# Attention in pairs of steps, the scans in two steps and the rotation back on GpSimd, in a hybrid MLA and S5 layer

## The chip, the cores and the metric

The kernel runs on one core of a Trainium2 chip. The metric is the time of one execution on the device in microseconds (us); lower is better. The engines are PE (TensorE), DVE (VectorE), ACT (ScalarE), POOL (GpSimd) and SP (SyncE, which issues most transfers). Each engine takes its instructions strictly in the order in which they are written, and waits for the others where data or a buffer is missing.

## The reference, cut to what matters

The layer takes x of 2048 positions by 1024 features in float32. After an RMS norm one product gives the inputs of two branches.

- Attention (MLA): four heads, a query of 128 features and 64 rotary ones for each, keys and values out of a common latent of 128 features, softmax over all 2048 positions.
- S5: 32 groups of 16 channels, each with a complex diagonal state of 64 in both directions; `h[t] = lam_bar h[t-1] + B u[t]`, `y = Re(C h) + D u`, then GELU and a gated unit.

```
s = einsum(qn, k_nope) + einsum(qr, k_rope);  p = softmax(s * scale);  o = p v
bu = einsum('sbgh,gph->sbgp', u, b_bar);  h = associative_scan(lam_bar, bu);  y += Re(einsum(h, c))
out = x + rmsnorm(concat(norm(o) * silu(g), norm(glu(gelu(y))) * silu(g2)) @ w_out)
```

## The kernel before

The program has three stages: the input product (phase 1), the attention loop with S5 beside it (phase 2), and the mixer with the output product (phase 3, `mixer`). The larger products take their operands in two parts, a high one in the type float32r and a low one, the rest.

The attention works on 32 units (`units`), a block of 256 queries by one head. A unit has eight steps: two halves of the queries (`qt`) by four blocks of 512 keys (`kb`). The loop over `t` runs these 256 steps and a tail of 15. In step `t` the queues receive, in this order:

- the second half of the row statistics of the last unit, if the step is the first of a unit (DVE: `L`, `lt`, `f`);
- `norm`: the exponentials of step t-9 are scaled (on ACT, L1143; on DVE, L1139, once the weights of phase 3 are being split);
- `s5_pre(t)`: what S5 has to do ahead of the scores;
- `scores`: five products into `sc` (PE, L1103 to L1107) and their maxima `nm` (DVE, L1108);
- `transp`: four transposes of step t-11 into `pt` (PE, L1151) and the high part `phi` (ACT, L1159);
- `expo`: `e` (ACT, L1114), in the last step of a unit the first half of the statistics;
- the low part `plo` (DVE, L1573);
- `av`: six products with the latent of step t-12 (PE, L1171 to L1173), after the eighth the copy `avs` (ACT, L1176); `unit_out` a step later;
- `s5_post(t)`, then a stage of the queries of the next block (`qprep`) or, near the end, of the weights of phase 3 (`out_weights`, `woh` on ACT at L1228).

A group of S5 is a routine (`group`) that goes one step at a time; a new group starts every seven steps, and takes fifteen. Its part around the change: the rotated inputs `ta`, `tb` (o = 6, counted from the group's start), their sum `X` (o = 7), four scans over 64 partitions each (o = 8, L1008 and L1009), the rotation back: `hc` on DVE (L1017) and `tb` on POOL (L1018) in o = 9, the difference `hc` on DVE (L1021) in o = 10, and PE's product with `hc` (L1034) in o = 14.

The rings that matter: score banks `psS` 2, transposes `psP` 2, `av` 1, `phi` and `plo` 2 each (`pp`), exponentials `e` 13 (`ep`). A new tile of a ring waits for the last reader of the one whose place it takes.

Of the kernel before, what the change touches and what calls it, by code (L numbers as in the profile page):

```python
# [21 lines left out]
P = 128  # L22
# [34 lines left out]
class Metered:  # L57
    """An engine that counts the elements it is given."""
# [13 lines left out]
class Scratch:  # L72
    """Temporaries of one shape, out of a ring of tiles of 512 (or, if small, 32) elements."""
# [22 lines left out]

def sincos(eng, sc, sin_out, cos_out, r):
    """sin and cos of r in about [-pi, pi], from those of r / 2."""
# [23 lines left out]
def exp_of(eng, sc, pool, out, x):  # L122
    """exp(x) in float32, exact at 0."""
# [24 lines left out]
def tile_hymba(ctx, tc, x, pos, inv_freq, pre_g, w_in, q_g, w_uqT, w_uqr, kv_g, w_ukT, w_uv, attn_g,  # L148
# [57 lines left out]
    # tables of the attention phase; those of S5 go through DRAM, by groups  # L206
# [11 lines left out]
    # ------------------------------------------------------------------ phase 1  # L218
# [51 lines left out]
    def turn(xt, t):  # L270
        """The tile's transpose, split, as tile t of a pair."""
# [34 lines left out]
    def gemm_t(nm, half):  # L306
        """Two blocks of 128 columns of a pair of tiles, with the columns in the partitions."""
# [43 lines left out]
    def s5_params():  # L351
# [37 lines left out]
        # F = (lam_bar - 1) / lam  # L389
# [17 lines left out]
        # powers of lam_bar, 0 .. T, in the order of each direction  # L407
# [29 lines left out]
        # phasors of chunk 32 i + 2 j + a: ph32 * (0..7) (+ phi), for a = 0, 1, and ph2 * (0..15)  # L437
# [13 lines left out]
        for nm, src in (("b", ph2), ("a", ph32)):  # L451
# [21 lines left out]
            # the backward direction turns the other way  # L473
# [11 lines left out]
        # B_bar = F B; B'' = B_bar e^{-i phi}; C' = lam_bar C  # L485
# [3 lines left out]
        def cm(orr, oi, ar, ai, xr_, xi_):  # L489
            """(orr, oi) = (ar + i ai)(xr + i xi), a over the last dimension."""  # L490
# [32 lines left out]
        # centre lag: Re(C B_bar) of both directions + D  # L523
        # (eight groups at a time: theirs are the blocks on the diagonal)
# [36 lines left out]
    def step():  # L561
        """A slice of the tables, of about BUDGET elements."""
# [15 lines left out]
    # absorbed weights: W_uq[h] W_uk[h]^T  # L578
# [23 lines left out]
    # the first tile is loaded and normed by halves  # L602
# [48 lines left out]
    # ------------------------------------------------------------------ phase 2  # L651
    # (the gate columns of the last two tiles run under its start)
# [5 lines left out]
    ep = pool(ph2, "ep", 13)  # L658
# [37 lines left out]
    # queries of a block of 256: each piece's last results are split a step later  # L696
# [74 lines left out]
    def both(*gens):  # L771
        """Step some routines in turn; what each returns."""
# [14 lines left out]
    # the gate columns of the last two tiles run under the start of the attention  # L787
# [58 lines left out]
    # S5  # L846
# [8 lines left out]
    def s5_load(q):  # L855
        """The tables of four groups."""
# [34 lines left out]
    def ops4(tile_, q_r, q_i, c1, c2):  # L891
        """The operands of tile_[., 2, s, h] = q_r[s] c1[., h] + q_i[s] c2[., h]."""
# [9 lines left out]
    def two(eng, tile_, tmp, *o):  # L902
        """The two products of a table; later they are added."""
# [18 lines left out]
    def k_build(q):  # L922
        """The kernels of the lags within a chunk, and their windows for each position."""
# [26 lines left out]
    def group(g):  # L950
        """A group of channels, a step at a time: what is ready first, what needs the PE last."""
        q, i = divmod(g, 4)
        f = S5[q]
        # (chunks in the order of their tiles: those of the even, then those of the odd places)
# [9 lines left out]
        # phasors over the chunks: -sin, cos, sin  # L964
# [39 lines left out]
        # (the states that enter the chunks; nothing enters the first, or the last backwards)  # L1004
# [6 lines left out]
        yield "pre"  # L1011
        yield "post"
# [4 lines left out]
        V.tensor_tensor(of_tiles(hc), g4, co, ALU.mult)  # L1017
# [3 lines left out]
        V.tensor_tensor(hc, hc, tb2, ALU.subtract)  # L1021
        yield "pre"
        yield "post"
# [20 lines left out]
    # when each group starts; the tables of the next four groups are made meanwhile  # L1044
# [52 lines left out]
    # attention  # L1097
    def scores(qo, st, i):
        qt, kb = i % 2, i // 2
        w = slice(qt * P, (qt + 1) * P)  # L1100
        c = slice(kb * 512, (kb + 1) * 512)
        ps = psS.tile([P, 512], F32, tag="s", name="sc")
        PE.matmul(ps, qo[:, 0, w], kT_h[:, c], start=True, stop=False)  # L1103
        PE.matmul(ps, qo[:, 0, w], kT_l[:, c], start=False, stop=False)  # L1104
        PE.matmul(ps, qo[:, 1, w], kT_h[:, c], start=False, stop=False)  # L1105
        PE.matmul(ps, qo[:, 2, w], krS[:, c], start=False, stop=False)  # L1106
        PE.matmul(ps, qo[:, 3, w], krS[:, c], start=False, stop=True)  # L1107
        V.tensor_reduce(st["nm"][:, qt, kb:kb + 1], ps, AX.X, ALU.max, negate=True)  # L1108
        st["s"] = ps

    def expo(st, i):
        qt, kb = i % 2, i // 2
        e = ep.tile([P, 512], F32, tag="e", name="e")
        A.activation(e, st.pop("s"), AF.Exp, bias=st["nm"][:, qt, kb:kb + 1], accum_out=st["L"][:, qt, kb:kb + 1])  # L1114
# [30 lines left out]
    def transp(st, j, tail=None):  # L1145
# [12 lines left out]
        ptf = pt.rearrange("p a b c -> p (a b c)")  # L1158
        A.activation(hi, ptf, AF.Copy)  # L1159
        st["p"][j] = hi, lo  # L1160
        return lo, ptf, hi
# [23 lines left out]
    # ------------------------------------------------------------------ weights of phase 3  # L1185
# [52 lines left out]
    # ------------------------------------------------------------------ phase 3  # L1238
    # (pairs of tiles, with the channels in the partitions up to W_out)
    def mixer():  # L1240
# [26 lines left out]
        def gelu(d):  # L1267
            """y <- 2 gelu(y), and its parts"""
# [38 lines left out]
        def part(d, src, h, c):  # L1307
            """hi and lo of half h of src, as blocks c .. of the products' operands"""
# [16 lines left out]
        def summed(d, sq):  # L1325
            """The sums of squares of the four channels in a partition"""
# [5 lines left out]
        def attn(d):  # L1332
            """o gated, and its parts"""
# [16 lines left out]
        def ssm(d):  # L1350
            """y <- 4 y sigmoid(. + b), gated into g, and its parts"""
# [37 lines left out]
        # the columns of the result in the parts that are worked on; the last tile ends in smaller ones  # L1389
# [11 lines left out]
        def comb(d, t, cs):  # L1401
            """Both branches by their factors, summed; the mean of the squares; times the gain"""
# [40 lines left out]
        # the first pairs, in small steps between those of the attention  # L1443
# [97 lines left out]
    late, qb = None, None  # L1541
    NLAG, LAG, AVLAG = 9, 11, 1
# [3 lines left out]
    TAIL = [[(0, "V"), (1, "A"), (2, "G"), (3, "G")], [(k, "G") for k in range(4, 8)]]  # L1546
    for t in range(8 * NU + LAG + AVLAG + 3):
        n, i = divmod(t, 8)
        # what the step before has made ready
        if n >= 1 and i == 0 and n - 1 < NU:  # L1550
            run(sts[n - 1]["stats"], 1)
        if t < 8 * NU and t >= NLAG:
            norm(sts[(t - NLAG) // 8], (t - NLAG) % 8, "A" if late is None else "V")
        s5_pre(t)
        # scores
        if n < NU:
            b, h = units[n]
            if i == 0:
                sts[n] = dict(e={}, p={}, nm=sm.tile([P, 2, 4], F32, tag="nm", name="nm"),
                              L=sm.tile([P, 2, 4], F32, tag="L", name="L"))  # L1560
            scores(qo[b][h], sts[n], i)
        m, j = divmod(t - LAG, 8)
        lo = transp(sts[m], j, p3) if 0 <= m < NU else None
        if n < NU:
            expo(sts[n], i)
            if t == 8 * NU - 1:
                V.tensor_tensor(lo[0], lo[1], f32(lo[2]), ALU.subtract)
                lo = None
            if i == 7:
                sts[n]["stats"] = stats(sts[n])  # L1570
                run(sts[n]["stats"], 1)
        if lo is not None:
            V.tensor_tensor(lo[0], lo[1], f32(lo[2]), ALU.subtract)  # L1573
        if t == 8 * NU - 1:
            norm(sts[NU - 2], 7, "V")
        elif 0 <= t - 8 * NU < len(TAIL):
            for k, eng in TAIL[t - 8 * NU]:
                norm(sts[NU - 1], k, eng)
        # (without scores in between, its operands take a step longer)
        lag = AVLAG + (t >= 8 * NU)  # L1580
        m, j = divmod(t - LAG - lag, 8)
        if 0 <= m < NU and t != 8 * NU:
            av(sts[m], j)
        m, j = divmod(t - LAG - lag - 1, 8)
        if 0 <= m < NU and j == 7:
            unit_out(*units[m], sts.pop(m))
        s5_post(t)
        # the queries of the next block
        if n < NU and b + 1 < 8:
# [89 lines left out]
```

## Time and profile before

| | us |
|---|---|
| median of 3 runs | 1434.57 (1433.16 to 1434.58) |
| span of the profiled execution | 1431.5 |
| attention loop, first to last exponential | 396.5 to 1170.6 |
| busy PE / DVE / ACT / POOL | 1359.6 / 1053.7 / 789.0 / 624.9 |

The profiled execution's own time is its span, from the first to the last instruction; the median of the runs lies 3.1 us above it. Matmuls overlap, so PE's busy time is not PE at its peak. An instruction's duration reaches some 0.08 us beyond the start of its neighbour on the same engine; what one costs is read from start to start.

### The profile page before, as it was taken

Reading aid. Unit: us, or ns where it says so; the run is one execution under the profiler, and the core shown is the slowest. Engines: PE = TensorE matmul, PEld = TensorE weight load, DVE = VectorE, ACT = ScalarE, POOL = GpSimd, SP = SyncE. Lnnn points to the kernel's source line nnn. Section 1 sums busy time; section 2 is a strip of 40 time slices with the busy share of each in tenths; the row PEclk is TensorE's granted clock in tenths of the full one; section 3 lists DMA queues with packets and bytes.
Section 4 is the critical chain, followed back from the end, with each engine's and each line's share of the span. In section 5 each row is a group of like instructions: output and inputs, shape, how many; then the busy total and the mean of one; then the engine's idle time right before and its main releaser. Section 6 shows DMA issues by size and latency. Waiting matters only on the chain.

```text
span 1431.5 us, 24291 instructions
## 1 busy us (share of the span) xinstructions
PE 1359.6 (95%) x9016; PEld 1221.6 (85%) x9016; DVE 1053.7 (74%) x1876; ACT 789.0 (55%) x1796; POOL 624.9 (44%) x616
## 2 busy tenths in 40 slices
PE   7999999999989999999999998999999989999998
PEld 7999999999968788887888887887888878788886
DVE  5456545332588888898989888988888895876774
ACT  6321222122457767767677676676677775544542
POOL 2102321233364655555556555645542695323340
PEclk9999999999999999999999999999999999999999
DMA  8322332442610110201102011020100345345432
GB/s 293 89 61 66 80 87 73 98 122 73 150 35 19 39 34 5 54 19 31 41 5 61 12 32 41 23 43 5 32 5 9 101 128 131 118 148 179 145 103 88
DMA packets 122133, 102.91 MB, mean 72 GB/s; under 512 B 14672, under 2 KB 107104, under 8 KB 122016
## 3 DMA queue, kind: packets, MB, share of 16 engines
q1 hardware_dynamic: 110384, 89.43, 22.3%
q0 software_dynamic: 2272, 7.62, 2.0%
q10 hardware_dynamic: 9360, 4.33, 1.5%
q8 instruction: 70, 1.15, 0.3%
q14 instruction: 47, 0.39, 0.1%
HBM read 63.80 MB, written 37.54 MB: 71 GB/s over the span
## 4 chain that ended last, share of the span: by engine, by line
PE 59%; DVE 26%; ACT 5%; issue 4%; POOL 2%; DMA 2%; SPq 1%; ACTq 0%; POOLq 0%; DVEq 0%
DVE plo L1573 5%; DVE nm L1108 4%; PE po L202 4%; PE po L203 4%; PE po L204 4%; PE pt L1151 3%; DVE hc L1017 3%; DVE G L1009 3%; DVE G L1008 3%; PE z_ga L203 2%; PE z_ga L204 2%; PE z_ga L202 2%; PE av L1173 2%; PE z_u L204 2%; PE z_u L202 2%
## 5 line engine op out<-in xcount | busy, mean ns | idle before, releaser
L1114 ACT ACTIVATE e<-sc,nm 128x512 f32<-128x512 f32 x256 | 176.4, 689 | 141.1 <-DVE nm L1108 139.8
L1573 DVE TENSOR_TENSOR plo<-pt,phi 128x512 fp32r<-128x512 f32 x255 | 175.0, 686 | 49.2 <-ACT phi L1159 46.3
L1159 ACT ACTIVATE phi<-pt 128x512 fp32r<-128x512 f32 x256 | 152.8, 597 | 72.9 <-PE pt L1151 72.4
L1108 DVE TENSOR_REDUCE nm<-sc 128x1 f32<-128x512 f32 x256 | 175.0, 683 | 17.6 <-PE sc L1107 15.6
L1173 PE MATMUL av<-plo,kn_h 128*128 128x256 f32 x512 | 150.6, 294 | 30.0 <-DVE plo L1573 29.5
L1171 PE MATMUL av<-phi,kn_h 128*128 128x256 f32 x512 | 165.7, 324 | 13.3 <-ACT avs L1176 13.2
L1143 ACT ACTIVATE e<-e,f 128x512 f32<-128x512 f32 x226 | 163.8, 725 | 1.5 <-DVE f L1132 1.5
L1151 PEld LDWEIGHTS pt<-ident,e 128*128 128x128 f32 x1024 | 127.8, 141 | 38.9 <-DVE e L1139 4.5
L1151 PE MATMUL pt<-ident,e 128*128 128x128 f32 x1024 | 154.8, 274 | 4.3 <-DVE e L1139 3.5
L1172 PE MATMUL av<-phi,kn_l 128*128 128x256 f32 x512 | 144.6, 282 | 0.0
L1173 PEld LDWEIGHTS av<-plo,kn_h 128*128 128x128 f32 x512 | 96.5, 189 | 40.1 <-DVE plo L1573 39.3
L1018 POOL TENSOR_TENSOR tb<-G,t 128x512 f32<-128x512 f32 x32 | 41.6, 1301 | 192.2 <-DVE G L1009 192.2
L1103 PE MATMUL sc<-kT_h,qo 128*128 128x512 f32 x256 | 114.7, 448 | 2.9 <-ACT e L1114 1.4
L1171 PEld LDWEIGHTS av<-phi,kn_h 128*128 128x128 f32 x512 | 97.6, 191 | 16.6 <-ACT avs L1176 16.5
L202 PE MATMUL po<-woh,ah 128*128 128x512 f32 (+1 forms) x264 | 102.6, 389 | 1.9 <-ACT u L1410 1.9
L203 PE MATMUL po<-wol,ah 128*128 128x512 f32 (+1 forms) x264 | 102.4, 388 | 0.0
L204 PE MATMUL po<-woh,al 128*128 128x512 f32 (+1 forms) x264 | 102.3, 388 | 0.0
L1104 PE MATMUL sc<-kT_l,qo 128*128 128x512 f32 x256 | 101.5, 396 | 0.0
L1106 PE MATMUL sc<-krS,qo 128*128 128x512 f32 x256 | 101.3, 396 | 0.0
L1107 PE MATMUL sc<-krS,qo 128*128 128x512 f32 x256 | 101.2, 395 | 0.0
L1105 PE MATMUL sc<-kT_h,qo 128*128 128x512 f32 x256 | 100.8, 394 | 0.0
L1172 PEld LDWEIGHTS av<-phi,kn_l 128*128 128x128 f32 x512 | 97.7, 191 | 0.0
(337 smaller groups left out, 4148.6 us busy)
## 6 DMA issues: line engine op xcount, KB each, us to landing
g_d<-gst SPq DMA_DIRECT2D x64, 128.0 KB, 2.0
g<-g_d SPq DMA_DIRECT2D x16, 512.0 KB, 5.7
xr<-in_x_dram SPq DMA_DIRECT2D x16, 512.0 KB, 6.7
xt<-in_x_dram SPq DMA_DIRECT2D x15, 512.0 KB, 3.8
out_dram<-res SPq DMA_DIRECT2D x15, 512.0 KB, 3.1
u_d<-ust ACTq DMA_DIRECT2D x64, 64.0 KB, 2.1
u<-u_d SPq DMA_DIRECT2D x64, 64.0 KB, 2.5
o_d<-o SPq DMA_DIRECT2D x32, 128.0 KB, 1.8
```

The source lines that it names most:

```text
L202: PE.matmul(ps, ahi, bhi, start=first, stop=False)
L203: PE.matmul(ps, ahi, blo, start=False, stop=False)
L204: PE.matmul(ps, alo, bhi, start=False, stop=last)
L1108: V.tensor_reduce(st["nm"][:, qt, kb:kb + 1], ps, AX.X, ALU.max, negate=True)
L1114: A.activation(e, st.pop("s"), AF.Exp, bias=st["nm"][:, qt, kb:kb + 1], accum_out=st["L"][:, qt, kb:kb + 1])
L1143: A.activation(e, e, AF.Copy, scale=f)
L1151: PE.transpose(pt[:, kk, qt, :], st["e"][qt, kt // 4][:, o:o + P], ident)
L1159: A.activation(hi, ptf, AF.Copy)
L1171: PE.matmul(o, kn_h[:, kt, :], hi[:, w], start=kt == 0, stop=False)
L1172: PE.matmul(o, kn_l[:, kt, :], hi[:, w], start=False, stop=False)
L1173: PE.matmul(o, kn_h[:, kt, :], lo[:, w], start=False, stop=kt == NT - 1)
L1573: V.tensor_tensor(lo[0], lo[1], f32(lo[2]), ALU.subtract)
```

## The change

The loop goes by pairs `p` of steps. In a pair the order is: the second half of the statistics; two norms (of pair p-4); `s5_pre(2p)`; the scores and maxima of both query halves for a block of keys; the eight transposes of pair p-5; both exponentials; the first half of the statistics; `s5_post(2p)`; a stage of the queries or weights; both `phi`; both `plo`; `unit_out`; the first `av` of pair p-6; `s5_pre(2p+1)`; the second `av`; `s5_post(2p+1)`; another stage of the queries or weights. Thus `phi` stands behind `e` and behind what S5 and the queries issue on ACT. The eight norms of the last unit are issued at once: two on DVE, two on ACT, four on POOL (before one, one and six). The ring `e` has 12 places; `phi` and `plo` keep 2.

In `group` the scans of the first component stand in o = 8 and those of the second in o = 9; both products of the rotation back are on POOL in o = 10, the difference on POOL in o = 11; PE's product stays in o = 14.

```diff
-    ep = pool(ph2, "ep", 13)
+    ep = pool(ph2, "ep", 12)
...
             V.tensor_tensor_scan(gt[64:P, o + 1:o + NC][:, ::-1], df[64:P], xm[64:P, r, 1:][:, ::-1], 0.0,
                                  ALU.mult, ALU.add)
-        yield "pre"
-        yield "post"
+            yield "pre"
+            yield "post"
...
-        V.tensor_tensor(of_tiles(hc), g4, co, ALU.mult)
+        G.tensor_tensor(of_tiles(hc), g4, co, ALU.mult)
         G.tensor_tensor(of_tiles(tb2), g4[:, ::-1], si, ALU.mult)
         yield "pre"
         yield "post"
-        V.tensor_tensor(hc, hc, tb2, ALU.subtract)
-        yield "pre"
-        yield "post"
+        G.tensor_tensor(hc, hc, tb2, ALU.subtract)
...
-    def scores(qo, st, i):
+    def scores(qo, st, k):
+        c = slice(k * 512, (k + 1) * 512)
+        st["s"] = []
+        for qt in range(2):
...
-        A.activation(hi, ptf, AF.Copy)
         st["p"][j] = hi, lo
-        return lo, ptf, hi
+        return pt.rearrange("p a b c -> p (a b c)"), hi, lo
...
-    NLAG, LAG, AVLAG = 9, 11, 1
+    NLAG, LAG, AVLAG = 4, 5, 6
...
-    for t in range(8 * NU + LAG + AVLAG + 3):
...
+    for p in range(4 * NU + AVLAG + 1):
+        n, k = divmod(p, 4)
+        t = 2 * p
+        tail = n >= NU
+        if k == 0 and n >= 1 and n - 1 < NU:
+            run(sts[n - 1]["stats"], 1)
+        if not tail and p >= NLAG:
+            for i in range(2):
+                m, kk = divmod(p - NLAG, 4)
+                norm(sts[m], 2 * kk + i, "A" if state[0] is None else "V")
+        elif p == 4 * NU:
+            for i, eng in enumerate(TAIL):
+                norm(sts[NU - 1], i, eng)
+        s5_pre(t)
+        if not tail:
...
+            scores(qo[b][h], sts[n], k)
+        m, kk = divmod(p - LAG, 4)
+        pts = [transp(sts[m], 2 * kk + i, p3) for i in range(2)] if 0 <= m < NU else []
+        if not tail:
+            for i in range(2):
+                expo(sts[n], 2 * k + i)
...
+        s5_post(t)
...
+            between(t)
+        for pt_, hi_, lo_ in pts:
+            A.activation(hi_, pt_, AF.Copy)
+        for pt_, hi_, lo_ in pts:
+            V.tensor_tensor(lo_, pt_, f32(hi_), ALU.subtract)
...
+            unit_out(*units[m], sts.pop(m))
+        m, kk = divmod(p - AVLAG, 4)
+        if 0 <= m < NU:
+            av(sts[m], 2 * kk)
+        s5_pre(t + 1)
+        if 0 <= m < NU:
+            av(sts[m], 2 * kk + 1)
+        s5_post(t + 1)
...
+            between(t + 1)
```

`between(t)` holds the stage of the queries or of the weights that stood at the end of a step, with the same conditions; in the tail a stage of the mixer takes its place.

## Rows read from the trace of the kernel before

**Rows 1.** The page: the span, and each engine's busy time, share and instructions.
```profile
span 1431.5 us, 24291 instructions
...
PE 1359.6 (95%) x9016; PEld 1221.6 (85%) x9016; DVE 1053.7 (74%) x1876; ACT 789.0 (55%) x1796; POOL 624.9 (44%) x616
```
**Rows 2.** Stages: length, busy us (instructions) of each engine, PE's clock, DMA.
```profile
436.00:1091.00 655.00, 615.34 (x4042) 540.05 (x4041) 579.38 (x986) 462.64 (x1087) 356.41 (x332) 0.99 0.12 27
1091.00:1114.00 23.00, 23.00 (x147) 20.19 (x146) 17.09 (x32) 18.10 (x42) 1.38 (x3) 1.00 0.06 12
1114.00:1172.00 58.00, 54.08 (x341) 46.57 (x339) 50.14 (x84) 42.38 (x96) 46.77 (x39) 1.00 0.39 112
```
**Rows 3.** Waits of PE's weight loads, 436 to 1091: us, times, longest.
```profile
PEld av L1173 <- DVE plo L1573: 34.8, 38, 2.8
PEld av L1171 <- ACT avs L1176: 15.6, 12, 2.0
```
**Rows 4.** Groups of DVE, 436 to 1091: busy us, mean ns, idle before.
```profile
L1017 DVE TENSOR_TENSOR hc<-G,t 128x512 f32<-128x512 f32 x30 | 50.0, 1667 | 0.0
L1009 DVE TENSOR_TENSOR_SCAN G<-tab,X 64x255 f32<-64x255 f32 x60 | 43.6, 727 | 0.8
...
L1021 DVE TENSOR_TENSOR hc<-hc,tb 128x512 f32<-128x512 f32 x30 | 39.9, 1329 | 2.5 <-POOL tb L1018 2.5
L1001 DVE TENSOR_TENSOR X<-ta,tb 128x512 f32<-128x512 f32 x30 | 22.1, 738 | 0.0
...
L996 DVE TENSOR_TENSOR ta<-px,t 128x512 f32<-128x512 f32 x30 | 20.6, 686 | 6.2 <-PE px L204 5.6 <-issue 0.3
...
L764 DVE TENSOR_TENSOR qo<-ptr,qo 128x128 fp32r<-128x128 f32 x56 | 12.2, 278 | 0.0
...
L1132 DVE TENSOR_TENSOR f<-f,lt 128x8 f32<-128x8 f32 x26 | 11.1, 428 | 0.9
...
L1130 DVE TENSOR_REDUCE lt<-L 128x2 f32<-128x8 f32 x26 | 4.2, 161 | 0.9
L720 DVE TENSOR_TENSOR zl<-ptq,zh 128x512 fp32r<-128x512 f32 x6 | 4.1, 680 | 0.0
```
**Rows 5.** Groups of ACT, 436 to 1091.
```profile
L1114 ACT ACTIVATE e<-sc,nm 128x512 f32<-128x512 f32 x209 | 144.1, 689 | 119.9 <-DVE nm L1108 118.8
```
**Rows 6.** Groups of POOL, 436 to 1091.
```profile
L975 POOL TENSOR_TENSOR t<-t,t3b 128x768 f32<-128x768 f32 x30 | 59.0, 1968 | 2.0
...
L1018 POOL TENSOR_TENSOR tb<-G,t 128x512 f32<-128x512 f32 x30 | 39.0, 1301 | 176.8 <-DVE G L1009 176.8
```
**Rows 7.** Timeline, 604 to 608, DVE and ACT: start, duration, engine, line.
```profile
604.39 0.68 DVE L1108 TENSOR_REDUCE nm<-sc 128x1 f32<-128x512 f32 x1
...
605.00 0.68 DVE L1573 TENSOR_TENSOR plo<-pt,phi 128x512 fp32r<-128x512 f32 x1
605.11 0.69 ACT L1114 ACTIVATE e<-sc,nm 128x512 f32<-128x512 f32 x1 [1.75 <-DVE nm L1108]
...
605.78 0.38 ACT L195 ACTIVATE wTh<-pw 128x256 fp32r<-128x256 f32 x1
...
606.66 0.59 ACT L1159 ACTIVATE phi<-pt 128x512 fp32r<-128x512 f32 x1
...
607.29 0.69 DVE L1573 TENSOR_TENSOR plo<-pt,phi 128x512 fp32r<-128x512 f32 x1
```
**Rows 8.** Timeline of PE, 1158 to 1161, first score product of two steps.
```profile
1158.25 0.40 PE L1103 MATMUL sc<-kT_h,qo 128*128 128x512 f32 x1
...
1160.57 0.40 PE L1103 MATMUL sc<-kT_h,qo 128*128 128x512 f32 x1
```
**Rows 9.** Groups of all engines, 1113 to 1172.
```profile
L1139 DVE TENSOR_SCALAR e<-e,f 128x512 f32<-128x512 f32 x22 | 17.1, 777 | 0.0
...
L1228 ACT ACTIVATE woh<-raw,ga 128x512 fp32r<-128x512 f32 x16 | 11.5, 721 | 5.3 <-DMA raw<-in_w_out_dram 5.3
...
L1132 DVE TENSOR_TENSOR f<-f,lt 128x8 f32<-128x8 f32 x2 | 1.9, 944 | 0.1
```

More of the change, by code (lines that the diff above doesn't have):

```diff
@@ L1095, in s5_post @@
                 live.remove(x_)
-    def scores(qo, st, i):
[L1099 to L1109, printed above, removed]
+    def scores(qo, st, k):
+        c = slice(k * 512, (k + 1) * 512)
+        st["s"] = []
+        for qt in range(2):
+            w = slice(qt * P, (qt + 1) * P)
+            ps = psS.tile([P, 512], F32, tag="s", name="sc")
+            PE.matmul(ps, qo[:, 0, w], kT_h[:, c], start=True, stop=False)
+            PE.matmul(ps, qo[:, 0, w], kT_l[:, c], start=False, stop=False)
+            PE.matmul(ps, qo[:, 1, w], kT_h[:, c], start=False, stop=False)
+            PE.matmul(ps, qo[:, 2, w], krS[:, c], start=False, stop=False)
+            PE.matmul(ps, qo[:, 3, w], krS[:, c], start=False, stop=True)
+            V.tensor_reduce(st["nm"][:, qt, k:k + 1], ps, AX.X, ALU.max, negate=True)
+            st["s"].append(ps)
     def expo(st, i):
@@ L1540, in tile_hymba @@
     sts = {}
-    late, qb = None, None
-    NLAG, LAG, AVLAG = 9, 11, 1
+    NLAG, LAG, AVLAG = 4, 5, 6
     QOFF = {0, 1, 2, 4, 5, 6}
@@ L1545, in tile_hymba, with between @@
     p3 = None
-    TAIL = [[(0, "V"), (1, "A"), (2, "G"), (3, "G")], [(k, "G") for k in range(4, 8)]]
-    for t in range(8 * NU + LAG + AVLAG + 3):
+    TAIL = "VAVAGGGG"
+    def between(t):
         n, i = divmod(t, 8)
[L1550 to L1554, printed above, removed]
+        late_, qb_, qn_ = state
         if n < NU:
@@ L1557, in tile_hymba @@
             b, h = units[n]
-            if i == 0:
+            if b + 1 < 8:
+                k = 8 * h + i
+                if k == 0:
+                    qb_, qn_ = qprep(b + 1, psQ, "q"), 0
+                held = qn_ % 2 == 1
+                if qb_ and (held if i == 3 else i != 4 and PLACE.get(t, (0, 0))[1] in QOFF):
+                    qn_ += 1
+                    try:
+                        next(qb_)
+                    except StopIteration as e_:
+                        qo[b + 1] = e_.value
+                        qb_ = None
@@ new lines, in between @@
+            if h == NH - 1 and i == 7:
+                assert b == 7 or b + 1 in qo
+                qo.pop(b)
+            if late_ is None and t >= START[NG] + 8 and b == 7:
+                s5x.close()
+                ph2q.close()
+                late_ = out_weights()
+        if late_ is not None:
+            next(late_, None)
+        state[:] = late_, qb_, qn_
+    state = [None, None, 0]
+    for p in range(4 * NU + AVLAG + 1):
[13 more added lines that the diff above has]
+        if not tail:
+            b, h = units[n]
+            if k == 0:
@@ L1559, in tile_hymba @@
                 sts[n] = dict(e={}, p={}, nm=sm.tile([P, 2, 4], F32, tag="nm", name="nm"),
                               L=sm.tile([P, 2, 4], F32, tag="L", name="L"))
[L1561 to L1569, printed above, removed]
+            scores(qo[b][h], sts[n], k)
@@ L1570, in tile_hymba @@
+        m, kk = divmod(p - LAG, 4)
[3 more added lines that the diff above has]
+                expo(sts[n], 2 * k + i)
+            if k == 3:
                 sts[n]["stats"] = stats(sts[n])
                 run(sts[n]["stats"], 1)
[L1572 to L1585, printed above, removed]
-            unit_out(*units[m], sts.pop(m))
-        s5_post(t)
-        if n < NU and b + 1 < 8:
-            k = 8 * h + i
-            if k == 0:
-                qb, qn = qprep(b + 1, psQ, "q"), 0
-            held = qn % 2 == 1
-            if qb and (held if i == 3 else i != 4 and PLACE.get(t, (0, 0))[1] in QOFF):
-                qn += 1
-                try:
-                    next(qb)
-                except StopIteration as e_:
-                    qo[b + 1] = e_.value
-                    qb = None
@@ L1601, in tile_hymba @@
-        if n < NU and h == NH - 1 and i == 7:
-            assert b == 7 or b + 1 in qo
-            qo.pop(b)
-        if late is None and t >= START[NG] + 8 and b == 7:
-            s5x.close()
-            ph2q.close()
-            late = out_weights()
-        if late is not None:
-            next(late, None)
-        if t == 8 * NU - 1:
-            assert next(late, "end") == "end"
+        s5_post(t)
+        if tail:
+            next(p3)
+        else:
+            between(t)
+        for pt_, hi_, lo_ in pts:
+            A.activation(hi_, pt_, AF.Copy)
@@ new lines, in tile_hymba @@
+        for pt_, hi_, lo_ in pts:
+            V.tensor_tensor(lo_, pt_, f32(hi_), ALU.subtract)
+        m, kk = divmod(p - AVLAG - 1, 4)
+        if 0 <= m < NU and kk == 3:
+            unit_out(*units[m], sts.pop(m))
+        m, kk = divmod(p - AVLAG, 4)
[5 more added lines that the diff above has]
+        s5_post(t + 1)
+        if tail:
+            next(p3)
+        else:
+            between(t + 1)
@@ L1612, in tile_hymba @@
+        if p == 4 * NU - 1:
+            assert next(state[0], "end") == "end"
             ph3w.close()
@@ L1615, in tile_hymba @@
             p3 = mixer()
-        if t >= 8 * NU:
-            next(p3)
+    next(p3)
     ph2.close()
```

3 lines of the change are left out of this document (1 added, 2 removed).

## The prediction

> **What bounds the kernel now.** I read the page first, then the span cut into stages, then the attention loop's waits, its groups of instructions and short pieces of the timeline.
>
> The page shows a span of 1431.5 us with PE busy 95% and DVE 74% [rows 1]. A busy PE is an average over stages, so the second view cuts the span. The change touches only the attention loop (about 396 to 1172) and the few steps behind it. In the long middle of the loop, 436 to 1091, where the S5 groups run beside it, DVE is busy 579 of 655 us (88%), PE 615, ACT 463, POOL 356 [rows 2]. 208 steps fall into it (the group of exponentials counts 209 with the two at the edges [rows 5]), so a step takes 3.15 us and a pair of steps 6.30.
>
> What does PE need alone? Its weight loads stood still for 34.8 us behind `plo` and 15.6 us behind `avs` [rows 3]; without these 50.4 us the stretch would be 604.6 us, 5.81 us a pair. So there are 0.49 us in each pair to be won, 51 us in all, and nothing beyond it: the change leaves PE's instructions as they are. A pair without S5 or query work needs 2 x 2.32 = 4.64 us, the distance of the first score matmuls of two neighbouring steps where PE did not wait [rows 8].
>
> Why does `plo` come late? DVE does it in its order, behind bursts of the S5 chain: four scans of 0.7 us in one step, then `hc` with a mean of 1.67 us and a second `hc` of 1.33 us, against 0.69 us for `ta` of the same 128x512 size [rows 4]. The two `hc` take 89.9 us of DVE in this stretch.
>
> **The change part by part.**
>
> *The rotation back on GpSimd.* DVE loses both `hc`: 1.67 + 1.33 = 3.0 us a group, one group in 3.5 pairs, 0.86 us a pair. POOL gains a product like `tb` (1.30 us, same shapes and reading order) and a subtraction for which `t` (1.97 us for 768 elements) gives 1.31 us [rows 6]: 2.6 us a group, some 78 us on an engine that is idle 300 us of the 655. The difference used to be made two steps after the scans and is now made three after their first half; PE wants it three steps later, 9 us. What POOL does in between is one sum of 1.97 us and, at times, a table of about 2 us, so I cost this at nothing; if POOL came too late, each us would be a us of PE.
>
> *The scans in two steps.* Same instructions, 1.4 us in each of two steps. When the first of the two steps is the second of a pair, both halves fall between the same two pairs, 2.8 us as before; so the burst is halved for every second group only.
>
> *Pairs of steps.* This is the dear part. Before, ACT did `phi` ahead of the step's `e`: it waited for no reduction of that step. Now the order on ACT is norm, norm, e0, e1, whatever the S5 step and the queries issue, phi0, phi1, and on DVE nm0, nm1, plo0, plo1, then the S5 work of the odd step and of the next even step, then the next nm0. Each engine works in order, so one chain goes round once a pair. From the timeline [rows 7]: nm to e 0.72 (604.39 to 605.11); e to the next ACT instruction 0.67 (605.11 to 605.78), twice; phi to plo 0.63 (606.66 to 607.29); plo to the next DVE instruction as nm to plo, 0.61 (604.39 to 605.00), twice. Sum 3.91 us. Between plo1 and the next nm0 comes what S5 keeps on DVE: `ta` and `tb` 0.60 each as neighbours, `X` 0.66, four scans 2.8, 4.7 us a group, 1.33 a pair. The row statistics are four DVE instructions, `f` with 0.43 and as much again for `L`, two of 0.16 [rows 4], 1.16 us in every fourth pair: 0.29; their `f` on ACT 0.05; the two norms now stand directly behind that `f` and hold e0 up to 0.5 us: 0.06. The S5 copies and splits of about 0.4 us [rows 7] that fall into the chain: 0.13. The queries' five DVE groups, from `qo` 12.2 to `zl` 4.1, sum to 38.1 us [rows 4], 0.37 a pair; what lies in the chain of it, with ACT copies, 0.27. Sum 3.91 + 1.33 + 0.29 + 0.05 + 0.06 + 0.13 + 0.27 = 6.04 us, above the 5.81 of PE. So the chain, not PE, sets the pace.
>
> Two further waits come with it. The ring for `phi` keeps two buffers, while two are written before the pair's products read the last two: phi0 now waits for the first `av` of its pair, phi1 for the second. As `av` stands at the end of PE's pair, this bites only where DVE is early. And there are two score buffers: the next pair's first scores wait for e0. For both I add 0.06, choosing low because the chain is the longer one in most pairs: 6.10. Bounds: 6.04 (no coupling) and 6.30 (0.26 us of coupling, half of what PE loses in a pair today).
>
> In return the wait for `avs` goes (15.6 us): its copy now has half a pair before the next unit's first `av`. That is inside the 6.10.
>
> Result for the middle: 104 pairs x (6.30 - 6.10) = 20 us less; from 0 to 27 us less by the bounds.
>
> *The last 23 steps before the mixer, 1114 to 1172.* Here the S5 work is over, the norms are on DVE (`e` 0.78 us mean, 22 times) and ACT also splits the output weights (`woh` 0.72 us) [rows 9]. A step takes about 2.5 us now (57 us), near PE's 2.32. With the change both norms stand between plo1 and nm0, 1.4 us as neighbours, and one `woh` stands between e1 and phi0, 0.67 as above: 3.91 + 1.4 + 0.67 = 6.0, and with the statistics (`f` 0.94 here, some 1.5 us in two of eleven pairs, partly beside ACT) 6.2 us a pair against 5.0: 11 x 1.2 = 13 us more. PE's 4.64 does not cover that. Bounds: with norms of 0.5 us 6 us more, with 1.2 us each 20 us more. Before, these norms stood beside PE's work and cost nothing.
>
> *The stretch 1091 to 1114* (4.5 pairs, now 5.1 us a pair, PE full [rows 2]): two of the pairs still have scans in the chain, 1.5 us more. *Fill and tail:* the eight norms of the last unit go out at once, two each on DVE and ACT, four on POOL (six before); as many steps of the mixer stand there. Cost 0, bounds 3 us to either side. The ring `e` has 12 places, six pairs, and a tile is turned five pairs after it is made: no wait. Loads and stores keep their number; they move by at most a step on SP's queue.
>
> POOL's load could slow DVE: statistics of 8 elements a row took 0.43 us on average though their neighbours of that size took 0.16. Were POOL a fifth busier, a fifth of that excess (0.5 us in each of 26 units, `f` and `L`) would be 2.7 us; I take nothing, and 4 us as the bound. The Trainium skill says under "SBUF — State Buffer", "Who interferes with whom", that a DVE instruction with two SBUF inputs blocks against a GpSimd instruction that reads SBUF. By it the pair `hc` and `tb`, started together, blocked each other, and gathering both on POOL frees DVE; the 1.67 against 0.69 us agrees.
>
> **Sum.** -20 + 1.5 + 13 + 0 = -5.5 us: span 1426.0. The runs' median lies 3.1 us above the profiled span: 1429.1 us.
>
> **The rivals.**
>
> *DVE was the bound and its relief pays in full.* For it: 88% busy, `plo` the largest wait of PE. Against it: the chain of 6.04 us. If it held, the middle would run at PE's 5.81: 51 us less, with the last steps 13 more about 38 less: 1397 us; half of that, 1415. The Trainium skill's "Perfetto Trace Analysis", "Identifying the Most-Contended Engine", says to improve the busiest engine first; by that rule alone this would be the outcome.
>
> *The chain is longer than I have it, and the kernel slower.* Place: nm0, e0, e1, phi0, plo0, plo1, S5, nm0. It decides from a mean of 6.16 us a pair in the middle, for then 104 x 0.14 = 14.5 us equal the loss at the end. At 6.30 to 6.40 the middle gives 0 or takes 10 us, the sum is +14 to +25: about 1452 us. For it: the sum leaves out queueing between chain and PE but for 0.06.
>
> *No measurable change*, the middle's gain eaten by the end: chain at 6.13 to 6.18: 1434 us.
>
> *POOL late for PE:* 1 us in each of 32 groups, 32 us more; with my gain 1461. Against it: the 9 us of room.
>
> **How the numbers follow.** A measurement of this kernel can tell about 0.2%, 2.9 us, from no change. My own case 0.50, of which 0.35 falls below -0.2%, 0.11 within and 0.04 above; its own range is 1420 to 1438. DVE relief in full 0.12, no change 0.11, longer chain 0.21, POOL late 0.06. Faster 0.47, same 0.22, slower 0.31. For 8 in 10 the range reaches half way into the first rival, 1412, and near the longer chain's time, 1449.
>
> **What the profile after would show.** Right: in the middle PE waits for `plo` at its transposes and for `e` at its scores instead of at `av`; the wait for `avs` is gone; DVE below 80% there, with idle time before `plo` put down to `phi`; `phi` idle behind `av` or `e`; a pair of 6.0 to 6.2 us. In the last 23 steps PE has gaps and the pair is about 6 us. Wrong: a middle at 5.8 (the chain does not bind), or PE waiting for `hc` of POOL, or last steps that stay near 5.0.

## The result and the profile after

| | before | after |
|---|---|---|
| median of 4 runs, us | 1434.38 (1433.16 to 1434.58) | 1489.42 (1486.47 to 1492.69) |
| ratio | 1 | 1.0386 (1.0369 to 1.0403) |
| span of the profiled execution, us | 1431.5 | 1490.9 |

The kernel became 3.9% slower, 55 us, where 5.5 us faster was forecast; the time lies above the range. Ratios compare runs in the faster of two states that the executions show; only the kernel with the pairs alone had a run in the slower one (1579.84 us at a clock of 0.84), and as that is the profiled one, its stages are not given below. The page after, its span and the busy time of the engines, answers [rows 1]:

```profile
span 1490.9 us, 24429 instructions
...
PE 1381.9 (93%) x9016; PEld 1240.1 (83%) x9016; DVE 984.7 (66%) x1812; ACT 783.8 (53%) x1798; POOL 680.2 (46%) x678
```

DVE lost 69 us of work, and yet the span grew by 59 us. No engine gained as much as that: the time is waiting. (PE's 22 us more of work are the same 9016 instructions, some of them at a lower clock.) Where it lies is read from the starts of `e` of the steps 0, 16, 224, 234 and 255 in both traces:

| us | step 0 to 16 | 16 to 224 (104 pairs) | 224 to 234 | 234 to 255 | behind it |
|---|---|---|---|---|---|
| before | 40.2 | 654.0 | 25.4 | 54.5 | 261.0 |
| after | 44.4 | 690.7 | 25.6 | 69.2 | 264.3 |
| difference | +4.2 | +36.7 | +0.2 | +14.7 | +3.3 |

The middle of the loop, the stretch with the scans' last pairs, and the last steps, as in [rows 2]: length, then busy us (instructions) of PE, PEld, DVE, ACT and POOL, PE's clock, DMA:

```profile
441.00:1132.00 691.00, 627.22 (x4040) 550.85 (x4040) 508.45 (x925) 458.03 (x1086) 410.02 (x392) 0.98 0.11 25
1132.00:1157.00 25.00, 24.91 (x155) 21.89 (x154) 17.08 (x33) 18.21 (x43) 3.92 (x5) 1.00 0.09 16
1157.00:1227.00 70.00, 56.29 (x326) 46.63 (x324) 50.27 (x79) 38.72 (x90) 45.29 (x38) 0.95 0.32 90
```

In the middle DVE's share fell from 88% to 74% (508 of 691 us), and PE stands for longer than before. A pair of steps takes 690.7 / 104 = 6.64 us, 6.29 before. PE's granted clock also fell: 30.7 us of the middle stand at its lower level, 1.2 GHz, in place of 6.8, and 6.8 us of the last steps in place of none. One such place: PE stood for `e`, began at full clock, and from 522.6 us was granted 0.50 of it:

```profile
521.88 0.50 PE L1102 MATMUL sc<-kT_h,qo 128*128 128x512 f32 x1 [3.08 <-ACT e L1113]
522.22 0.40 PE L1103 MATMUL sc<-kT_l,qo 128*128 128x512 f32 x1
...
523.21 0.63 PE L1106 MATMUL sc<-krS,qo 128*128 128x512 f32 x1
```

The waits of the middle, where [rows 3] showed `plo` and `avs` ahead of PE (us in total, times, longest):

```profile
ACT e L1113 <- DVE nm L1107: 125.4, 87, 4.4
DVE plo L1612 <- ACT phi L1610: 107.9, 67, 3.2
ACT e L1142 <- DVE f L1131: 69.9, 26, 5.6
...
PE sc L1102 <- ACT e L1113: 36.3, 27, 3.2
...
DVE nm L1107 <- PE sc L1106: 18.2, 29, 1.7
ACT phi L1610 <- PE av L1169: 11.1, 18, 1.1
...
PE ptr L758 <- ACT o L1179: 8.3, 6, 2.4
```

ACT waits for DVE at `e`, DVE for ACT at `phi`: the two engines hand the work to and fro, and neither is full. PE, last in the row, waits at its scores, since a score buffer comes free only when `e` has read it. The waits for `avs` and `plo` at `av` are gone. One pair shows the round; first DVE (start, duration, line; "x2" is two instructions in one line):

```profile
604.84 1.28 DVE L1107 TENSOR_REDUCE nm<-sc 128x1 f32<-128x512 f32 x2
607.79 1.29 DVE L1612 TENSOR_TENSOR plo<-pt,phi 128x512 fp32r<-128x512 f32 x2 [1.67 <-ACT phi L1610]
608.99 0.67 DVE L1008 TENSOR_TENSOR_SCAN G<-tab,X 64x255 f32<-64x255 f32 x1
609.68 0.69 DVE L1009 TENSOR_TENSOR_SCAN G<-tab,X 64x255 f32<-64x255 f32 x1
610.38 0.42 DVE L746 TENSOR_TENSOR ta<-psr,ropec 128x256 f32<-128x256 f32 x1
610.72 0.41 DVE L747 TENSOR_TENSOR tb<-psr,ropes 128x256 f32<-128x256 f32 x1
611.05 0.67 DVE L1008 TENSOR_TENSOR_SCAN G<-tab,X 64x255 f32<-64x255 f32 x1
611.74 1.61 DVE L1009 TENSOR_TENSOR_SCAN G<-tab,X 64x255 f32<-64x255 f32 x1
613.38 1.29 DVE L1107 TENSOR_REDUCE nm<-sc 128x1 f32<-128x512 f32 x2
```

and ACT in the same pair:

```profile
605.55 0.69 ACT L1113 ACTIVATE e<-sc,nm 128x512 f32<-128x512 f32 x1 [2.54 <-DVE nm L1107]
...
606.23 0.68 ACT L1113 ACTIVATE e<-sc,nm 128x512 f32<-128x512 f32 x1
...
606.89 0.38 ACT L1035 ACTIVATE y<-py 128x256 f32<-128x256 f32 x1
607.15 1.09 ACT L1610 ACTIVATE phi<-pt 128x512 fp32r<-128x512 f32 x2
...
614.11 0.69 ACT L1113 ACTIVATE e<-sc,nm 128x512 f32<-128x512 f32 x1 [4.37 <-DVE nm L1107]
```

`nm` at 604.84, `e` at 605.55 and 606.23, a copy of S5, `phi` at 607.15, `plo` at 607.79, then DVE's S5 and query work for 4.4 us, and only then the next `nm` at 613.38. While DVE scans, ACT has no `nm` to work on (4.37 us idle); while ACT works on `e`, DVE has no `phi` (1.67 us). In this pair, with four scans and query work in it, the round took 8.54 us.

The rotation back arrived on POOL as costed, 1.29 us for the product and as much for the difference, against the 1.30 and 1.31 of the prediction. Groups of DVE and POOL in the middle, to [rows 4 and 6]:

```profile
L1009 DVE TENSOR_TENSOR_SCAN G<-tab,X 64x255 f32<-64x255 f32 x60 | 46.8, 780 | 0.8
L1008 DVE TENSOR_TENSOR_SCAN G<-tab,X 64x255 f32<-64x255 f32 x60 | 44.4, 740 | 0.3
...
L1017 POOL TENSOR_TENSOR hc<-G,t 128x512 f32<-128x512 f32 x30 | 38.8, 1292 | 178.3 <-DVE G L1009 141.6 <-PE sc L1106 27.4 <-PE av L1169 4.5
L1021 POOL TENSOR_TENSOR hc<-hc,tb 128x512 f32<-128x512 f32 x30 | 38.7, 1290 | 0.5
...
L1001 DVE TENSOR_TENSOR X<-ta,tb 128x512 f32<-128x512 f32 x30 | 28.5, 950 | 0.2
```

In the last steps the round is the same, with the norms in it, and ACT's `woh` between `e` and `phi`. DVE there:

```profile
1187.08 1.29 DVE L1612 TENSOR_TENSOR plo<-pt,phi 128x512 fp32r<-128x512 f32 x2 [2.02 <-ACT phi L1610]
1188.28 2.22 DVE L1138 TENSOR_SCALAR e<-e,f 128x512 f32<-128x512 f32 x2
1190.43 1.28 DVE L1107 TENSOR_REDUCE nm<-sc 128x1 f32<-128x512 f32 x2
1193.71 1.29 DVE L1612 TENSOR_TENSOR plo<-pt,phi 128x512 fp32r<-128x512 f32 x2 [2.01 <-ACT phi L1610]
```

From `plo` to `plo` 6.63 us, 2.15 of it the two norms (1188.28 to 1190.43). The clock was at its full level there.

### The profile page after: what moved, and what is told of

The parts are those of the page before. It is cut to its first block, busy times and chain, and to the rows that moved or that the text cites. A ratio compares the mean times of both kernels' runs of the same rounds, so it can differ in the third digit from the quotient of the medians.

```text
span 1490.9 us, 24429 instructions
## 1 busy us (share of the span) xinstructions
PE 1381.9 (93%) x9016; PEld 1240.1 (83%) x9016; DVE 984.7 (66%) x1812; ACT 783.8 (53%) x1798; POOL 680.2 (46%) x678
## 4 chain that ended last, share of the span: by engine, by line
PE 32%; DVE 12%; ACT 8%; issue 4%; DMA 1%; SPq 1%; POOL 1%; ACTq 0%; DVEq 0%; POOLq 0%
PE po L202 3%; PE po L204 3%; PE po L203 3%; ACT e L1113 3%; PE pt L1150 3%; ACT phi L1610 2%; DVE plo L1612 2%; DVE nm L1107 2%; PE sc L1102 2%; DVE G L1009 2%; PE sc L1103 2%; PE sc L1104 2%; PE sc L1106 2%; PE sc L1105 2%; DVE G L1008 1%
## 5 line engine op out<-in xcount | busy, mean ns | idle before, releaser
L1612 DVE TENSOR_TENSOR plo<-pt,phi 128x512 fp32r<-128x512 f32 x256 | 167.7, 688 | 172.6 <-ACT phi L1610 137.8
L1142 ACT ACTIVATE e<-e,f 128x512 f32<-128x512 f32 x228 | 154.0, 736 | 78.1 <-DVE f L1131 78.1
L1107 DVE TENSOR_REDUCE nm<-sc 128x1 f32<-128x512 f32 x256 | 166.8, 684 | 24.7 <-PE sc L1106 22.9
L1168 PE MATMUL av<-phi,kn_h 128*128 128x256 f32 x512 | 157.5, 308 | 0.0
L1610 ACT ACTIVATE phi<-pt 128x512 fp32r<-128x512 f32 x256 | 142.4, 602 | 15.0 <-PE av L1169 11.3
L1150 PEld LDWEIGHTS pt<-ident,e 128*128 128x128 f32 x1024 | 120.6, 143 | 29.8 <-DVE plo L1612 14.0
L1150 PE MATMUL pt<-ident,e 128*128 128x128 f32 x1024 | 138.9, 277 | 6.2 <-DVE plo L1612 6.1
L1017 POOL TENSOR_TENSOR hc<-G,t 128x512 f32<-128x512 f32 x32 | 41.3, 1292 | 200.2 <-DVE G L1009 163.5
L1102 PEld LDWEIGHTS sc<-kT_h,qo 128*128 128x128 f32 x256 | 50.5, 197 | 73.6 <-ACT e L1113 64.1
L1106 PE MATMUL sc<-krS,qo 128*128 128x512 f32 x256 | 104.5, 408 | 0.0
L1105 PE MATMUL sc<-krS,qo 128*128 128x512 f32 x256 | 104.4, 408 | 0.0
```

What stands on the lines that cost most here:

```text
L1107: V.tensor_reduce(st["nm"][:, qt, k:k + 1], ps, AX.X, ALU.max, negate=True)
L1142: A.activation(e, e, AF.Copy, scale=f)
L1150: PE.transpose(pt[:, kk, qt, :], st["e"][qt, kt // 4][:, o:o + P], ident)
L1168: PE.matmul(o, kn_h[:, kt, :], hi[:, w], start=kt == 0, stop=False)
L1610: A.activation(hi_, pt_, AF.Copy)
L1612: V.tensor_tensor(lo_, pt_, f32(hi_), ALU.subtract)
```

## The experiments

Theory C says: the place of `phi` behind `e` closes a round nm, e, phi, plo, S5, nm through DVE and ACT in their orders, and this round sets the pace. The rivals are the rotation and the scans (POOL late, or in DVE's way), the pairing as such, the ring of `phi`, and the place of the norms.

| kernel | median, us | ratio to before | middle, us | last 21 steps, us |
|---|---|---|---|---|
| S5 part alone | 1404.95 | 0.981 (0.9793 to 0.9827) | 623.9 | 55.0 |
| pairs alone | 1539.13 | 1.0736 (1.0712 to 1.076) | | |
| rotation alone | 1400.58 | 0.9778 (0.9762 to 0.9795) | 621.6 | 53.7 |
| `phi` first | 1440.03 | 1.0052 (1.0037 to 1.0067) | 654.9 | 56.5 |
| `phi` first, norms behind `e` | 1449.21 | 1.011 (1.0094 to 1.0126) | 666.7 | 56.4 |
| norms behind `plo` | 1521.54 | 1.0615 (1.0595 to 1.0635) | 719.6 | 71.6 |
| four `phi` | 1485.9 | 1.0364 (1.0348 to 1.0379) | 685.6 | 70.0 |
| pairs, scans in one step | 1491.01 | 1.0405 (1.0381 to 1.0428) | 685.7 | 69.4 |
| `phi` first, norms a pair later | 1423.81 | 0.9938 (0.9922 to 0.9954) | 639.4 | 55.6 |
| steps, `phi` behind `e` | 1576.4 | 1.1004 (1.098 to 1.1028) | 776.1 | 66.7 |

Middle is the stretch from `e` of step 16 to that of step 224 in the profiled execution, last steps those from 234 to 255.

**The two halves of the change.** The S5 part alone: the loop of before with the routine `group` of after.

```diff
         V.tensor_tensor_scan(...)
-        yield "pre"
-        yield "post"
+            yield "pre"
+            yield "post"
...
-        V.tensor_tensor(of_tiles(hc), g4, co, ALU.mult)
+        G.tensor_tensor(of_tiles(hc), g4, co, ALU.mult)
...
-        V.tensor_tensor(hc, hc, tb2, ALU.subtract)
...
+        G.tensor_tensor(hc, hc, tb2, ALU.subtract)
```

> The loop of before, step by step, with the S5 part of the change alone (scans in two steps, both products and the difference of the rotation back on GpSimd). Theory C (the pair's chain nm0, e0, e1, phi0, plo0, plo1, S5, nm0 costs the time): the S5 part is a gain by itself, since DVE loses 3.0 us a group and phi stays ahead of e; of the 0.49 us that PE loses in a pair of steps about half comes back, 25 us less than before: about 1410 us (1395 to 1425). Rival P (the work on GpSimd costs the time, by blocking DVE's scans, X and statistics): 1450 us or more.

Measured 1404.95 us, by its ratio 27 us below before. The pairs alone: the loop of after, the routine `group` of before.

> The loop by pairs with the S5 chain of before (four scans in one step, both hc on DVE). Theory C: DVE's 3.0 us a group come back into the chain, 0.8 us a pair in 110 pairs: about 1489 + 80 = 1570 us (1540 to 1590). Rival P: without the extra work on GpSimd the loss is gone, 1435 to 1460 us.

Measured 1539.13 us, by its ratio 105 us above before; just under the 1540 that theory C had as its least. So the S5 part is worth 27 us in the loop by steps and 50 in that by pairs (1.0736 to 1.0386; theory C had 80), and the pairs cost 105 us without it and 83 with it (0.981 to 1.0386). A rotation that comes late on POOL, or a net loss by it, is out as the cause.

**The rotation without the split of the scans**, in the loop of before (only the last two edits of the diff above):

> The loop of before with the rotation back on GpSimd alone; the four scans stay in one step. Theory C: most of what the S5 part gives, since 3.0 of its us a group go and only the burst of 2.8 us stays: about 1415 us (1400 to 1430). Rival P: 1450 us or more.

Measured 1400.58 us, the fastest kernel of this study. The gain of the S5 part is the rotation's; the split of the scans adds nothing to it (with the split the time was 4 us longer: 1403.6 to 1406.15 against 1399.4 to 1402.67). PE's waits in the middle, 436 to 1057 (its products' own; before they were 26.5 and 12.8 us, and those of its weight loads stand in [rows 3]):

```profile
PE av L1173 <- DVE plo L1573: 10.8, 15, 2.7
PE av L1171 <- ACT avs L1176: 3.7, 5, 1.5
```

And the loop of pairs with the scans in one step:

> The changed kernel with the four scans in one step again (rotation back on GpSimd). Theory C: the scans are in the chain wherever they stand, so within 8 us of 1489. If the halved burst were worth something in pairs: 1500 us or more.

Measured 1491.01 us, 1.6 us from the changed kernel: there too the split is worth nothing that can be told.

**The place of `phi`.** In the changed kernel both `phi` are issued ahead of both `e`; four buffers for them, so that they need not wait for `av` of their own pair (`avs` goes down to one buffer to make room).

```diff
+        for pt_, hi_, lo_ in pts:
+            A.activation(hi_, pt_, AF.Copy)
         if not tail:
             for i in range(2):
                 expo(sts[n], 2 * k + i)
...
-        for pt_, hi_, lo_ in pts:
-            A.activation(hi_, pt_, AF.Copy)
...
-            hi = pp.tile([P, 512], F32R, tag="phi", name="phi")
+            hi = pp.tile([P, 512], F32R, tag="phi", name="phi", bufs=4)
...
```

> The changed kernel with both phi ahead of both e on ACT, and four buffers for phi so that they wait for no av of their pair (one buffer fewer for avs makes the room). plo stays where it is. Theory C: the chain is cut between e1 and phi0, PE sets the pace again at about 5.9 us a pair instead of 6.64 in the middle (77 us less) and about 5.2 instead of 6.6 in the last 11 pairs (15 us less): about 1400 us (1385 to 1425). Rival P, or a loss by the order of PE itself: within 15 us of the changed kernel's 1489.

Measured 1440.03 us: some 48 us come back, and the last steps are back at 56.5 us; but 40 us more than theory C had it, outside the range of either side. Some of its waits in the middle:

```profile
ACT e L1142 <- DVE f L1131: 71.9, 25, 5.7
...
DVE plo L1612 <- PE av L1170: 42.2, 34, 2.7
...
DVE wTl L196 <- ACT wTh L195: 34.5, 21, 2.8
PE sc L1102 <- ACT e L1113: 31.9, 21, 3.4
```

The norms of a unit's first pair stand on ACT ahead of everything, and wait for `f` of the statistics, which DVE makes only at the pair's start; `e` comes late behind them and PE's scores with it. The four buffers alone, in the order of after:

> The changed kernel with four buffers for phi (one fewer for avs), the order unchanged. Theory C: phi waits 11 us for av, and e1 to phi0 is 1.72 us in the pairs where both px and py stand before av against 0.85 to 1.07 elsewhere; without that wait some 10 to 25 us less, about 1472 us. Rival (the ring of two, not the order on ACT, is what makes phi late): 1450 us or less, as with phi first.

Measured 1485.9 us, where theory C had 1472: the ring (with one `avs` buffer fewer) is worth some 3 us at most, as the two intervals overlap, the order of `phi` the other 45.

**The norms' wait for `f`.** First, the norms put behind both `e`, with `phi` first:

```diff
-        if not tail and p >= NLAG:
-            for i in range(2):
-                m, kk = divmod(p - NLAG, 4)
-                norm(sts[m], 2 * kk + i, "A" if state[0] is None else "V")
         s5_pre(t)
...
                 sts[n]["stats"] = stats(sts[n])
                 run(sts[n]["stats"], 1)
+        if not tail and p >= NLAG:
+            for i in range(2):
+                m, kk = divmod(p - NLAG, 4)
+                norm(sts[m], 2 * kk + i, "A" if state[0] is None else "V")
```

> The kernel with phi ahead of e and four buffers for phi, and its norms issued behind both e instead of at the pair's start. What was left there: PE waits 29.8 us for e at its scores, in 20 waits, and ACT's norms wait 66.6 us for the f of the statistics, in 23 waits, ahead of phi and e. Theory C2 (the norms of a unit's first pair, directly behind f, hold up e and so the scores): 25 to 30 us less than that kernel's 1440, about 1412 us. Rival (the rest is the order of PE by pairs, with av as the last of a pair): within 8 us of 1440.

Measured 1449.21 us, 9 us more than with `phi` first alone, instead of 28 less. ACT no longer stands for `f`, and PE's wait at the scores was halved, from 31.9 to 16.2 us, as theory C2 had it. But PE now stood 21.8 us for `o` (the unit's output, copied by ACT) at the queries' products, in place of 4.9, and 8.5 us for `plo` at its transposes, in place of 0.2; DVE's wait for the high part of S5's weights nearly doubled, from 34.5 us.

```profile
PE sc L1102 <- ACT e L1113: 16.2, 14, 3.1
PE ptr L758 <- ACT o L1179: 8.8, 7, 1.8
...
DVE wTl L196 <- ACT wTh L195: 63.4, 30, 3.8
```

Second, in the changed kernel, the same four lines behind the two `plo`:

> The changed kernel with its norms behind phi and plo instead of at the pair's start; phi stays behind e. Theory C: nm0 to e0 takes 1.03 us in the first pair of a unit and 0.72 in the second, so 0.3 us in 26 pairs, 8 us, leave the chain: about 1481 us (1474 to 1489). If the wait for f (67 us on ACT) were itself the cause: 1440 us or less.

Measured 1521.54 us, 32 us more than the changed kernel, where 8 less were expected: theory C's account of the norms missed as well. ACT's waits for `nm` grew from 125.4 to 229.1 us, and PE's for `o` at the queries' products from 8.3 to 17.4 us:

```profile
ACT e L1113 <- DVE nm L1107: 229.1, 118, 6.5
...
PE ptr L758 <- ACT o L1179: 17.4, 7, 3.5
```

By these waits the norms hold up, in either place, what stands behind them in the pair; that is argued, and which wait makes the 32 us no run shows. Third, with `phi` first again, the norms where they were, but of the pair before (p-5), when `f` has long been there (the edits against the kernel with `phi` first):

```diff
-    NLAG, LAG, AVLAG = 4, 5, 6
+    NLAG, LAG, AVLAG = 5, 5, 6
...
         elif p == 4 * NU:
+            for i in (6, 7):
+                norm(sts[NU - 2], i, "V")
```

> The kernel with phi ahead of e took 1440.0 us, its middle 654.9 us, and in it ACT still stood 66.6 us (23 times) with a norm in front of the f of the statistics. Here the norms of a unit are issued a pair later (pair p-5, transposed in the same pair). Theory F: this wait is what is left; without it the middle comes near that of the loop by steps, 625 to 635 us, and the time near 1415 us. Rival: the wait for f only stands where another would stand in its place (the chain runs DVE, ACT, DVE anyway), and PE's transposes now wait for fresh norms: 1435 to 1445 us.

Measured 1423.81 us: 16 us less than with `phi` first alone, 0.6% faster than before. The wait for `f` is gone, and PE's wait at the scores was halved:

```profile
PE sc L1102 <- ACT e L1113: 17.0, 13, 3.2
```

So theory F holds for 16 of the 25 us that it named; the middle stayed at 639.4 us, above its 625 to 635.

**`phi` behind `e` without pairs.** The fastest kernel, by steps, with one edit: `phi` of a step behind its `e`.

```diff
-        A.activation(hi, ptf, AF.Copy)       # in transp, ahead of expo
...
             expo(sts[n], i)
+        if lo is not None:
+            A.activation(lo[2], lo[1], AF.Copy)
```

> The loop by steps with the rotation back on GpSimd (1400.6 us), and phi issued behind the step's e, as one edit. Theory C (the chain nm, e, phi, plo, next nm through two engines in order): a step becomes 0.72 + 0.67 + 0.63 + 0.61 + 1.06 (the S5, statistics and query work of DVE, half a pair's) = 3.7 us against 2.99, so 208 steps give some 145 us more, the last 23 some 35 more: about 1580 us, at least 1500. Rival (the pairing itself, its bursts on PE and the rings, not the place of phi, costs the time): 1400 to 1420 us.

Measured 1576.4 us, 176 us more than the fastest kernel, for the order of two instructions. The middle is 776.1 / 208 = 3.73 us a step; the sum by theory C was 3.7. The last steps gained 13 us, not the 35 of the expectation. Its stage and its largest waits there:

```profile
438.00:1214.00 776.00, 679.73 (x4034) 570.77 (x4033) 499.81 (x924) 458.08 (x1085) 406.80 (x392) 0.95 0.10 23
```

```profile
ACT e L1114 <- DVE nm L1108: 314.0, 198, 6.2
DVE plo L1575 <- ACT phi L1566: 260.0, 205, 1.5
...
PEld av L1170 <- ACT phi L1566: 82.6, 56, 4.4
```

The same two waits as in the changed kernel, now in nearly every one of 208 steps. With this order the pairing as such is no loss: it makes the round once where steps make it twice, and with the same S5 part took 1491 us where steps took 1576.

## Why the prediction was wrong

**The mechanism was right, the size of the round too small.** The prediction had the order of ACT as the dear part, named the round nm0, e0, e1, phi0, plo0, plo1, S5, nm0, and gave the slower kernel as a rival of its own ("the chain is longer than I have it"), with 6.30 to 6.40 us a pair. Measured are 6.64. The step that failed is the sum of the round, "6.04 us", with the "0.06" for coupling: both too small. The 6.64 lie above even the longer-chain rival, which had 1452 us. The parts of the sum, as means from start to start over the 104 pairs of the middle (the terms for statistics, copies and queries put where they fall):

| | predicted | measured |
|---|---|---|
| nm0 to e0, with the norms' wait for `f` | 0.72 + 0.06 = 0.78 | 0.825 |
| e0 to e1 | 0.67 | 0.771 |
| e1 to phi0, with `f` and the S5 copies | 0.67 + 0.05 + 0.13 = 0.85 | 1.08 |
| phi0 to plo0 | 0.63 | 0.633 |
| plo0 to plo1 | 0.61 | 0.636 |
| plo1 to the next nm0: plo, S5, statistics, queries | 0.61 + 1.33 + 0.29 + 0.27 = 2.50 | 2.697 |
| sum | 6.04 | 6.64 |

What the 0.60 us are, by the rows above:
- Coupling with PE: DVE's `nm` stood 18.2 us for scores, `phi` 11.1 us for `av` of its pair, 29.3 us or 0.28 us a pair; predicted 0.06, with 0.26 as the bound. The prediction took the mean of the round and put it above PE's mean (6.04 against 5.81). But pairs differ: from plo1 to nm0 a tenth of them took under 1.0 us and a tenth over 4.05. Where the round is short PE is the longer, where S5 fills it PE waits. The mean of the longer of two is more than the longer of two means; that two score buffers are too few to even this out is argued, no run had a third.
- S5 on DVE: scans, `X`, `ta` and `tb` took 1.51 us a pair from start to start in place of 1.33 (`X` 0.88 and a scan 0.78 us on average, predicted 0.66 and 0.70). In the kernel before the same instructions took 1.40, so 0.07 us was missed in reading, and 0.11 came with the change: nine of 30 `X` and ten of 120 scans took over 0.9 us, with POOL at work beside them. The prediction put the cost of POOL's greater load at nothing, with 4 us as the bound; these are 11 us.
- Most of the rest is ACT's copies and splits between e1 and phi0 (0.12) and the norms behind `f` (0.05).

So the middle lost 37 us in place of winning 20: 57 of the 65 us by which the forecast span was missed.

PE's lower clock is a cost that the prediction did not name ("5.81 of PE" is at nearly full clock). The rounds give no sign that it sets the pace: of the 104 rounds the 15 with over 0.5 us at 1.2 GHz took 6.04 us on average, the others 6.74; in the loop by steps with `phi` behind `e`, 31 such steps took 3.75 us, the others 3.73.

**The last steps** were forecast with 13 us more, and it was 14.7 (over 21 steps, forecast over 23). The term "1.4 as neighbours" for the two norms was too small: they took 2.15 us, beside POOL's work on the output weights.

**The stretch 1091 to 1114**: 1.5 us more forecast, 0.2 measured. **Fill and tail** at 0 with 3 us to either side: 4.2 and 3.3 us more, together 7.5, outside the bound. No run was made to find out which of the moved steps these belong to.

**The rotation back** went as costed: 1.29 us twice on POOL, no wait of PE for `hc`. In the loop of before it pays 32 us (0.9778): the relief of DVE, which the prediction had as a rival for the whole change ("pays in full": 1397 us; half: 1415), happens to this part alone (1400.6 us), and the other edit of the same diff takes it away. That 1397 lies so near is luck: it is 51 us off the middle and 13 more at the end, and the run has 32.4 off the middle and the end as before. One reading of the prediction was wrong: that `hc` and `tb`, "started together", blocked each other. In none of the 32 groups did the first `hc` run beside `tb`, whose time is 1.30 us before and after; in most it waited for POOL's next instruction (see the last section).

The Trainium skill's "Perfetto Trace Analysis", "Identifying the Most-Contended Engine", says to improve the engine with the highest occupancy first. For the rotation the runs agree; the whole change lowers DVE's share in the middle from 88% to 74% and is 3.9% slower, so that occupancy alone does not decide here.

**What the profile was to show.** Right: PE waiting for `e` at its scores, the wait for `avs` gone, DVE below 80% with idle time before `plo` put down to `phi`, gaps of PE at the end. Not foreseen: PE's products of the queries (`ptr`, `psq`) wait for `o` of the unit before, 8.3 and 6.8 us. Not borne out: that PE waits for `plo` at its transposes (0.7 us, 3.9 at their weight loads), and the length of a pair.

**Open.** With `phi` first and the norms a pair later, the loop of pairs is still 23 us behind the fastest kernel by steps, 18 of them in the middle (639.4 against 621.6). PE's 17.0 us at the scores are of that size, and a third score buffer would tell; it was not tried. The lower clock is the smaller part: 13.7 us of that middle stand at 1.2 GHz, and the eight pairs with over 0.5 us of it took 6.45 us, the others 6.13, some 2.6 us in all. Why the norms in the two later places cost time is open too.

## What to carry to other kernels

Where two in-order engines hand each tile to and fro, write down the round trip of one loop turn in issue order before looking at busy shares: one instruction placed behind the reduction of its own turn (`phi` behind `e`) cost 176 us of 1400 here, and left ACT 59% and DVE 64% busy in the middle of the loop. When such a sum comes near the length of another engine's turn, compare them turn by turn, not as means, and do not count the difference of the means as won (here 0.28 us a pair were lost to it, with two score buffers between them). When one diff holds an edit that relieves an engine and one that reorders a loop, run each alone: here one alone was 2.2% faster, the other alone 7.4% slower.

## What the runs showed of the hardware

A DVE instruction whose two inputs lie in SBUF took up to three times as long beside POOL in these traces, and one that reads PSUM did not change. Duration ns, shortest, median and longest of the same instruction; the kernel before, with `hc` on DVE:

```profile
L1017 DVE TENSOR_TENSOR hc<-G,t x32: 678/2007/2370, 423.6 to 1097.4; 128x512 f32<-128x512 f32 x32
```

and the changed kernel:

```profile
L1001 DVE TENSOR_TENSOR X<-ta,tb x31: 681/689/1953, 444.6 to 1135.0; 128x512 f32<-128x512 f32 x31
...
L1009 DVE TENSOR_TENSOR_SCAN G<-tab,X x62: 685/686/1826, 446.3 to 1141.7; 64x255 f32<-64x255 f32 x62
...
L1138 DVE TENSOR_SCALAR e<-e,f x22: 475/1040/1575, 1155.9 to 1224.1; 128x512 f32<-128x512 f32 x22
...
L1612 DVE TENSOR_TENSOR plo<-pt,phi x238: 680/691/695, 443.4 to 1222.5; 128x512 fp32r<-128x512 f32 x119
```

`plo`, with one input in PSUM, keeps to 680 to 695 ns in all its places; `hc`, both inputs in SBUF, takes 678 ns or about 2007. What decides is which of the two began first. Of the 31 `hc` (L1017) of the kernel before that start after 440 us, 23 found a POOL instruction under way, most often the product `t` (L971) that had begun 0.02 us earlier; they ended 0.55 us after it did, and took 1.97 us on average. For the other eight none was under way beyond their first 0.1 us, and they took 0.68, also where POOL began 0.16 us later. In those cases it was POOL that took longer: `qd` 1.66 us, 1.28 elsewhere. The scan, and a scaling by one value a row (`e` times `f`), behave alike (the scaling ended 0.28 us after POOL's instruction), while 114 of the 238 `plo` lay almost wholly within POOL's work and kept their time. The Trainium skill's "SBUF — State Buffer", "Who interferes with whom", has the rule: DVE's second read port is GpSimd's, so an instruction with two SBUF inputs contends with a GpSimd instruction that reads SBUF. The rows of `hc`, `X` and `plo` agree.
